# Retention moved beside its gate's block, its gated output kept in the gate's tiles, banks' release estimated, delays set anew

## Chip, core and metric

One core of a Trainium2 chip runs the whole program. The metric is the device time of one execution in microseconds (us), the median of several runs. PE is TensorE (matmuls), DVE is VectorE, ACT is ScalarE, POOL is GpSimd, SP issues most DMAs.

## The reference

Two layers over x (512 tokens x 1024). Each layer normalises h, projects it, runs four mixers of 512 columns, gates each with silu of a projection of its own, and adds the out-projection of all four to h. All is float32.

```python
for l in range(DEPTH):
    u = rmsnorm(h, norm_w[l])
    ret_p, diff_p, ssd_p, ml_p = split_cols(u @ w_in[l], (RET_COLS, DIFF_COLS, SSD_COLS, MLSTM_COLS))
    ret_out  = retention_mixer(rope(rq), rope(rk), rv) * silu(rz)     # chunks of 128 tokens, a state between
    diff_out = diff_attention_mixer(dq, dk, dv, lam) * silu(dz)
    ssd_out  = _rms(ssd_mixer(conv(xbc), dt) * silu(sz)) * ssd_norm_w
    ml_out   = mlstm_mixer(conv(mqk), mv, mo, gates) * silu(mz)       # its gates by a scan over 4 chunks
    h = h + concat([ret_out, diff_out, ssd_out, ml_out]) @ w_out[l]
return rmsnorm(h, final_norm_w)
```

## The kernel before

**Tiles.** Tokens lie in 4 tiles (t) of 128 on the partitions. Every weight block of 512 columns is loaded (`raw`) and split into a high part (`whi`, made by ACT, L327) and a low rest (`wlo`, made by DVE, L329). A product is three matmuls: `whi` with the high part of the other operand, `whi` with its low part, `wlo` with its high part. A projection block (`proj_tok`, `proj_feat`) is 96 matmuls of 128x512 in 4 PSUM tiles `pspj`; `uh`, `ul` are the parts of the normalised input, `mh`, `ml` those of a mixer's transposed output, which the out-projection (`out_proj`) multiplies. Such a block is called by its name: `rz` is the projection of retention's gate, `s` the out-projection of the SSD mixer, and so on.

**Order on PE.** PE's order is written out by the program itself, and Tile's scheduler orders the other engines. `drive` runs through the blocks in the order of the list `ORDER`. A clock `self.clk` advances by an estimate with every matmul. The mixers and their finishers are generators that are put beside the blocks: what they yield (a delay out of the table `W`) says after how much of that clock their next piece is put between the block's groups of three matmuls. `pause(key)` holds one until `key` is in the set `done`. The delays thus stand for the time that DVE, ACT and POOL take between two pieces on PE; if a delay is too short for what they take, PE waits.

**Banks.** PSUM has 8 banks. `free` puts a bank back with the clock at which its last reader was issued, and `psum` takes the one with the earliest such time. A matmul that gets a bank whose reader has not run yet waits for it.

**The pieces that the change touches.**
- Mixer mLSTM: `gates` scans over 4 chunks and transposes what DVE made (L695, L696; delays g1 to g4). `mlstm` starts m0 after the block `mk`; for each chunk a score matmul (`psS<-ft,ft`), a decay product on DVE (L760 by ACT to L767), then after mB the value matmuls (`psacc<-v,w`).
- SSD: score product on DVE (L874), value matmuls, then `fin_s`: normalised on DVE (L933), after sF the transposes.
- Differential attention (`diff`): a head's output lies in bank `o`; its last reader is L1106, and after dF its transposes follow.
- Retention (`ret`): for each chunk scores, decay product (L958), after rC the value matmuls, squares (L1002), a reciprocal root on POOL (L217), scaling (L1010). Its finisher `fin` multiplies by the gate on POOL (L842) into the w tile `mix`, and after rF `emit` transposes it on PE into a bank `psS`, and `finish_mix` makes `mh` (L547, ACT) and `ml` (L548, DVE) of that, which lie in 4 buffers each: the first tile of `r` takes those of the first tile of `s`.

Retention stands behind `rz` in `ORDER`, so its four chunks lie between the matmuls of the blocks `s` and `r`.

Of the kernel before, what the change touches and what calls it, by code (L numbers as in the profile page):

```python
# [15 lines left out]
ALU = mybir.AluOpType  # L16
# [5 lines left out]
NT = S // P  # L22
# [23 lines left out]


ORDER = ["mv", "gates", "mq", "mk", "mlstm", "mo", "mz", "dk", "dq", "diff", "dv", "dz", "m", "xs", "bc", "ssd", "d",
         "rqk", "sz", "rv", "rz", "ret", "s", "r"]


QS = 4


W = {'norm': 9.0, 'g1': 1.5, 'g2': 7.3, 'g3': 1.8, 'g4': 10.4, 'mB': 1.8, 'mC': 1.3, 'mN': 5.0, 'mF': 9.6, 'sB': 10.2,
     'sN': 0.0, 'sF': 6.1, 'rC': 2.3, 'rN': 0.0, 'rF': 9.8, 'dT': 9.14, 'dN': 1.0, 'dM': 3.0, 'dV': 6.68, 'dF': 15.46,
     'm0': 5.3, 's0': 8.8, 'dT1': 0.6, 'dN1': 1.0, 'hp': 100, 'he': 100, 'hr': 50, 'hd': 50, 'dS': 4.7, 'dQ': 6.0,
     'ha': 50}


# [31 lines left out]
class Trunk:  # L92
# [81 lines left out]
        self.bank[id(p)] = p, b  # L174
        return p

    def free(self, *ps):

        for p in ps:
            q, b = self.bank.pop(id(p))  # L180
            assert q is p
            heapq.heappush(self.banks, (self.clk, b))


    def setup(self):
# [235 lines left out]
    def proj_tok(self, name, evac, w=None, toks=range(NT), order=None):  # L421
        w = w or self.load_block(name)
        steps = [(t, k, parts) for t in toks for k, parts in order] if order else \
                [(t, k, (0, 1)) for t, k in self.steps_of(list(toks), name != "mv")]
        banks, n = {}, {}
        for t, k, parts in steps:
            if t not in banks:
                yield from self.wait(("u", self.l, t))
                banks[t] = self.psum("pj")
                n[t] = 0  # L430
            p = banks[t]
            ts_ = slice(t * P, (t + 1) * P)
            for part in parts:
                for u in (self.uh,) if part else (self.uh, self.ul):
                    n[t] += 1
                    self.mm(p, lhsT=u[:, k, ts_], rhs=w[k][part], start=(n[t] == 1), stop=(n[t] == 3 * KD))
            yield
            if n[t] == 3 * KD:
                evac(t, p)
                self.free(p)  # L440
                self.done.add((name, self.l, t))

    def proj_feat(self, name, evac):
        w = self.load_block(name)
        banks = {}
        for f, k in self.steps_of(range(4), True):
            p = banks[f] if k else banks.setdefault(f, self.psum("pj"))
            fs = slice(f * P, (f + 1) * P)
            hi, lo = w[k][0][:, fs], w[k][1][:, fs]
            self.mm(p, lhsT=hi, rhs=self.uh[:, k, :], start=(k == 0), stop=False)  # L450
            self.mm(p, lhsT=hi, rhs=self.ul[:, k, :], start=False, stop=False)
            self.mm(p, lhsT=lo, rhs=self.uh[:, k, :], start=False, stop=(k == KD - 1))
            yield
            if k == KD - 1:
                evac(f, p)
                self.free(p)


    def ev_silu(self, dst, tag, bufs, nwt=None):
# [81 lines left out]
    def finish_mix(self, mix):  # L541

        nc = self.nc
        p = self.tr4([mix[:, j * P:(j + 1) * P] for j in range(4)])
        mh = self.t("mh", [P, 512], F32R, bufs=4)
        ml = self.t("ml", [P, 512], F32R, bufs=4)
        nc.scalar.copy(out=mh, in_=p)  # L547
        nc.vector.tensor_tensor(out=ml, in0=p, in1=mh.bitcast(F32), op=ALU.subtract)  # L548
        self.free(p)
        return mh, ml  # L550

    def out_proj(self, g, mixt, tok_outer=False, after=None, cut=False, heads=False):
        nc = self.nc
        gi = GROUPS[g]
        w = [[x for q in range(2) for x in self.split_w(self.wout[self.l, gi, half, :, 2 * q:2 * q + 2, :], 2 * half + q)]
             for half in range(2)]
        l = self.l
        order = [(t, hf) for t in range(NT) for hf in range(2)] if tok_outer else \
                [(t, hf) for hf in range(2) for t in range(NT)]
        for t, hf in order:  # L560
            if hf == 0 or not tok_outer:
                yield from self.wait((g, l, t))
            m = lambda t, k: [x[:, t * P:(t + 1) * P] for x in mixt[k]] if heads else \
                [x[:, k * P:(k + 1) * P] for x in mixt[t]]
            cuts = self.cuts if cut and t == NT - 1 else (0, 512, D)
            for c0, c1 in zip(cuts, cuts[1:]):
                if c0 // 512 != hf:
                    continue
                bank = self.psum("pj")
                p = bank[:, 0:c1 - c0]  # L570
                cs = slice(c0 - hf * 512, c1 - hf * 512)
                for k in range(4):
                    hi, lo = w[hf][k]
                    mh, ml = m(t, k)
                    self.mm(p, lhsT=mh, rhs=hi[:, cs], start=(k == 0), stop=False)
                    self.mm(p, lhsT=ml, rhs=hi[:, cs], start=False, stop=False)
                    self.mm(p, lhsT=mh, rhs=lo[:, cs], start=False, stop=(k == 3))
                    yield
                hs = self.h[t][:, c0:c1]
                nc.vector.tensor_tensor(out=hs, in0=p, in1=hs, op=ALU.add)  # L580
                self.free(bank)
            if tok_outer and hf == 1:
                self.spawn(after(t))

# [157 lines left out]
    def mlstm(self, v, th, zs, q, k, res):  # L742
# [5 lines left out]
        for t in range(NT):  # L748
# [16 lines left out]
                self.mm(s[:, h * P:(h + 1) * P], lhsT=k[h][:, ts_], rhs=q[h][:, ts_])  # L765
            pt = self.pg()
            nc.vector.scalar_tensor_tensor(pt, s, sc, w, ALU.mult, ALU.mult)  # L767
            self.free(s)
            if t < NT - 1:
                kt = self.tr4([k[h][:, ts_] for h in range(4)])  # L770
                kw = self.pg()
# [1 line left out]
                                               kt.rearrange("p (h d) -> p h d", h=4), sc,  # L773
                                               self.bc(self.ws[:, t, :], P), ALU.mult, ALU.mult)
                self.free(kt)
            yield W["mB"]
            yield from self.pause(("mo", l, t))
            num = [self.psum("acc"), self.psum("acc")]
            for h in range(4):
# [25 lines left out]
            for j in range(2):  # L805
                nc.vector.scalar_tensor_tensor(g[:, j * 256:(j + 1) * 256].rearrange("p (h e) -> p h e", h=2),
                                               th[t][:, j * 256:(j + 1) * 256].rearrange("p (h e) -> p h e", h=2),
                                               1.0, nv[j][:, :, 0:128], ALU.add, ALU.mult)
            self.free(*num)
            r = self.sm([P, 4])  # L810
            nc.vector.tensor_tensor(out=r, in0=den, in1=self.em[:, t, :], op=ALU.max)
            nc.vector.reciprocal(out=r, in_=r)
# [24 lines left out]
        yield W["mF"]  # L837
        self.emit(l, t, "m", mix, res)

    def fin(self, l, t, g, mix, res, zs, key, w):  # L840
        yield from self.pause((key, l, t))
        self.nc.gpsimd.tensor_tensor(out=mix, in0=mix, in1=zs[t], op=ALU.mult)  # L842
        yield w
        self.emit(l, t, g, mix, res)


    def ssd(self, xs, bm, cm, zs, res):
# [5 lines left out]
        for t in range(NT):  # L853
# [12 lines left out]
            for g in range(2):  # L866
# [8 lines left out]
                                        in1=cb[:, g * P:(g + 1) * P].unsqueeze(1).to_broadcast([P, 4, P]),  # L875
                                        op=ALU.mult)
                es.append(e)
            self.free(cb)
            if t < NT - 1:
                pb = self.tr4([bm[g][:, ts_] for g in range(2)])  # L880
                bt = self.t("bt", [P, 256], bufs=2)
# [56 lines left out]
    def retention(self, qk, v, zs, res):  # L938
# [6 lines left out]
        for t in range(NT):  # L945
# [64 lines left out]
                nc.vector.tensor_tensor(out=v4(mix)[:, j::2, :], in0=ob[j][:, 0:256].rearrange("p (h d) -> p h d", h=2),  # L1010
                                        in1=self.bc(f[:, j::2], P), op=ALU.mult)
            self.free(*ob)
            self.spawn(self.fin(l, t, "r", mix, res, zs, "rz", W["rF"]))
            yield W["rN"]


# [11 lines left out]
    def diff(self, q, k, v, zs, res):  # L1028
        nc = self.nc
        l = self.l  # L1030
        for h in range(4):
# [6 lines left out]
            for t in range(NT):  # L1038
                n = (t + 1) * P
                ts_ = slice(t * P, n)  # L1040
                nm = self.sm([P, 2])
                pe = [self.pg(), self.pg()]
                sj = [self.psum("S"), self.psum("S")]

                for i, (a, b) in enumerate(((0, 0), (0, 1), (1, 0))):
                    for j, s in enumerate(sj):
                        own = slice(j * 64, j * 64 + 64)
                        self.mm(s[:, 0:n], lhsT=qp[a][own, ts_], rhs=k[h][b][own, 0:n], start=(i == 0), stop=(i == 2),
                                share=0.5)
                with self.tc.high_priority(W["hd"]):  # L1050
                    for j, s in enumerate(sj):
                        nc.vector.tensor_tensor(out=s[:, ts_], in0=s[:, ts_], in1=self.mlow, op=ALU.add)  # L1052
                        nc.vector.tensor_reduce(out=nm[:, j:j + 1], in_=s[:, 0:n], axis=AX.X, op=ALU.max, negate=True)  # L1053
                        nc.scalar.activation(pe[j][:, 0:n], s[:, 0:n], AF.Exp, bias=nm[:, j:j + 1],  # L1054
                                             accum_out=r[:, t, j:j + 1])
                        self.free(s)
                    rr = self.sm([P, 1])
                    nc.vector.reciprocal(out=rr, in_=r[:, t, 1:2])
                    nc.vector.scalar_tensor_tensor(ca[:, t:t + 1], rr, r[:, t, 0:1], self.nlam, ALU.mult, ALU.mult)
                    a = pe[0]  # L1060
                    nc.vector.scalar_tensor_tensor(a[:, 0:n], pe[1][:, 0:n], ca[:, t:t + 1], pe[0][:, 0:n],
                                                   ALU.mult, ALU.add)
                self.spawn(self.diff_av(l, t, h, a, o, v), W["dT"] + t * W["dT1"])
                yield W["dN"] + t * W["dN1"]
# [21 lines left out]
    def diff_fin(self, h, o, r, zs, res, l):  # L1086
# [6 lines left out]
        for t in range(NT):  # L1093
# [11 lines left out]
        mix = self.pg()  # L1105
        nc.vector.tensor_tensor(out=mix.rearrange("p (t d) -> p t d", t=NT), in0=o.rearrange("p (t d) -> p t d", t=NT),  # L1106
                                in1=self.bc(f, P), op=ALU.mult)
        self.free(o)
        for t in range(NT):
            yield from self.pause(("dz", l, t))  # L1110
            ts_ = slice(t * P, (t + 1) * P)
# [169 lines left out]
```

## Time and profile before

| what | value |
|---|---|
| median of 3 runs | 1050.69 us (1049.36 to 1051.6) |
| profiled execution | 1054.91 us, its span 1053.1 us |
| PE busy | 1024.8 us, 97% of the span |
| DVE, ACT, POOL busy | 701.9, 470.6, 192.7 us |
| mean granted clock of PE | 0.993 |

The span is what the trace shows; 1.8 us of the profiled execution lie around it. A busy PE is one with a matmul in it, at whatever clock. Layer 0 ends its last out-projection at about 535 us; the places of layer 1 lie some 516 us behind those of layer 0.

### The profile page before, as it was taken

The page shows a single profiled execution, that of the slowest core. Times are in us where ns is not written, and L with a number is a line of the kernel's source. Part 1 is how long each engine was busy: PE and PEld are TensorE (multiplying, and loading weights), DVE is VectorE, ACT ScalarE, POOL GpSimd, SP SyncE. Part 2 cuts the span into 40 slices and gives each one's busy share as a digit, 9 for nine tenths or more (in the row PEclk, how much of TensorE's full clock was granted, in tenths as well). Part 3 has the DMA queues.
Part 4 walks back from the last instruction along what each step waited for, and adds up shares of the span by engine and source line. Part 5 has one row for each costly group of instructions (what it writes and reads, how often), then busy time and mean ns, then how long its engine had stood idle before and what let it go on. Part 6 is the DMA issues. An engine that isn't in the chain of part 4 may idle for free.

```text
span 1053.1 us, 14255 instructions
## 1 busy us (share of the span) xinstructions
PE 1024.8 (97%) x5116; PEld 835.5 (79%) x5116; DVE 701.9 (67%) x1501; ACT 470.6 (45%) x1050; POOL 192.7 (18%) x221
## 2 busy tenths in 40 slices
PE   7999999999999999999999999999999999999997
PEld 6778888877778888787887788887777878888876
DVE  5587686567787868445556867666686786872554
ACT  4444336645455344432353443475444453643322
POOL 3000152102111342004000013320121112510121
PEclk8999999999999999999999999999999999999999
DMA  7323322322212332431122423223231223232202
GB/s 294 106 79 113 101 66 86 100 81 81 79 42 92 101 89 89 128 106 65 40 81 81 125 82 96 80 80 102 70 104 46 80 84 117 85 113 83 80 21 81
DMA packets 39143, 95.54 MB, mean 91 GB/s; under 512 B 3592, under 2 KB 16520, under 8 KB 38944
## 3 DMA queue, kind: packets, MB, share of 16 engines
q1 hardware_dynamic: 38064, 93.18, 28.5%
q10 hardware_dynamic: 1008, 1.44, 0.4%
q8 instruction: 40, 0.66, 0.3%
q14 instruction: 31, 0.25, 0.1%
HBM read 92.47 MB, written 2.15 MB: 90 GB/s over the span
## 4 chain that ended last, share of the span: by engine, by line
PE 85%; DVE 7%; DMA 3%; ACT 2%; issue 1%; POOL 0%; SPq 0%; POOLq 0%; DVEq 0%; ACTq 0%
PE pspj L114 70%; PE psacc L114 6%; PE psS L114 5%; PE psS L118 4%; DMA raw<-in_w_in_dram 2%; DVE wlo L329 2%; DVE e L509 1%; DVE s L1053 1%; ACT whi L327 1%; DMA cst<-in_consts_dram 1%; ACT w L1054 1%; DMA raw<-in_w_out_dram 0%; DVE h L580 0%; POOL s L217 0%; DVE psS L1052 0%
## 5 line engine op out<-in xcount | busy, mean ns | idle before, releaser
L329 DVE TENSOR_TENSOR wlo<-raw,whi 128x512 fp32r<-128x512 f32 x298 | 215.2, 740 | 69.5 <-ACT whi L327 67.1
L327 ACT CAST whi<-raw 128x512 fp32r<-128x512 f32 x300 | 178.6, 619 | 112.1 <-PE pspj L114 53.9
L114 PE MATMUL pspj<-whi,uh 128*128 128x512 f32 x512 | 208.2, 407 | 0.9 <-ACT whi L327 0.6
L114 PE MATMUL pspj<-whi,ul 128*128 128x512 f32 x512 | 200.9, 392 | 0.0
L114 PE MATMUL pspj<-wlo,uh 128*128 128x512 f32 x512 | 200.4, 393 | 0.0
L114 PE MATMUL pspj<-uh,whi 128*128 128x512 f32 x448 | 179.5, 401 | 0.0
L114 PE MATMUL pspj<-uh,wlo 128*128 128x512 f32 x448 | 174.8, 390 | 0.0
L114 PE MATMUL pspj<-ul,whi 128*128 128x512 f32 x448 | 174.7, 390 | 0.0
L114 PE MATMUL pspj<-whi,mh 128*128 128x512 f32 (+1 forms) x260 | 107.6, 414 | 8.0 <-DVE ml L548 4.2
L114 PEld LDWEIGHTS pspj<-whi,uh 128*128 128x128 f32 x512 | 97.0, 189 | 23.0 <-issue 2.0
L114 PEld LDWEIGHTS pspj<-wlo,uh 128*128 128x128 f32 x512 | 96.7, 189 | 21.0
L114 PEld LDWEIGHTS pspj<-whi,ul 128*128 128x128 f32 x512 | 97.1, 190 | 18.0
L114 PE MATMUL pspj<-whi,ml 128*128 128x512 f32 (+1 forms) x260 | 103.1, 396 | 0.2 <-DVE ml L548 0.2
L114 PE MATMUL pspj<-wlo,mh 128*128 128x512 f32 (+1 forms) x260 | 102.8, 395 | 0.0
L114 PEld LDWEIGHTS pspj<-uh,wlo 128*128 128x128 f32 x448 | 84.1, 188 | 18.3
L114 PEld LDWEIGHTS pspj<-uh,whi 128*128 128x128 f32 x448 | 84.3, 188 | 17.1 <-issue 0.7
L114 PEld LDWEIGHTS pspj<-ul,whi 128*128 128x128 f32 x448 | 84.3, 188 | 15.8
L217 POOL TENSOR_TENSOR s<-s,nhalf 128x4 f32<-128x4 f32 (+1 forms) x44 | 36.1, 820 | 328.1 <-DVE s L1101 126.5
L509 DVE SCALAR_TENSOR_TENSOR e<-pspj,cvh,e 128x511 f32<-128x511 f32 (+2 forms) x90 | 67.0, 745 | 14.3 <-ACT e L507 13.2
L114 PEld LDWEIGHTS pspj<-whi,mh 128*128 128x128 f32 x260 | 49.6, 191 | 21.3 <-issue 5.0
L580 DVE TENSOR_TENSOR h<-pspj,h 128x512 f32<-128x512 f32 (+1 forms) x65 | 43.6, 676 | 33.9 <-PE pspj L114 33.6
L527 ACT ACTIVATE e<-pspj 32x512 f32<-32x512 f32 x96 | 56.6, 589 | 19.3 <-PE pspj L114 18.0
(213 smaller groups left out, 1359.0 us busy)
## 6 DMA issues: line engine op xcount, KB each, us to landing
raw<-in_w_in_dram SPq DMA_DIRECT2D x118, 512.0 KB, 3.9
raw<-in_w_out_dram SPq DMA_DIRECT2D x32, 512.0 KB, 3.4
bcm<-adr SPq DMA_DIRECT2D x16, 256.0 KB, 3.9
bcm<-gdr SPq DMA_DIRECT2D x8, 256.0 KB, 3.4
out_dram<-z SPq DMA_DIRECT2D x7, 256.0 KB, 2.0
h<-in_x_dram SPq DMA_DIRECT2D x3, 512.0 KB, 7.9
rows<-in_rows_dram SPq DMA_DIRECT2D x2, 592.0 KB, 9.0
cst<-in_consts_dram SPq DMA_DIRECT2D x1, 1035.0 KB
```

Source lines behind the costliest of these rows:

```text
L114: self.nc.tensor.matmul(out, lhsT=lhsT, rhs=rhs, start=start, stop=stop, **kw)
L118: self.nc.tensor.transpose(out, src, self.ident if ident is None else ident)
L217: self.nc.gpsimd.tensor_tensor(out=out, in0=m, in1=self.nhalf[:, :n], op=ALU.pow)
L327: (nc.vector.tensor_copy if vector else nc.scalar.copy)(out=hi, in_=raw)
L329: eng.tensor_tensor(out=lo, in0=raw, in1=hi.bitcast(F32), op=ALU.subtract)
L509: nc.vector.scalar_tensor_tensor(acc[:, s:], p[:, 0:S - s], w[:, 3 - s:4 - s], acc[:, s:], ALU.mult, ALU.add)
L527: nc.scalar.activation(x[q * 32:q * 32 + 32, :], p[o * 32:o * 32 + 32, :], AF.Copy, scale=scale)
L580: nc.vector.tensor_tensor(out=hs, in0=p, in1=hs, op=ALU.add)
L1053: nc.vector.tensor_reduce(out=nm[:, j:j + 1], in_=s[:, 0:n], axis=AX.X, op=ALU.max, negate=True)
L1054: nc.scalar.activation(pe[j][:, 0:n], s[:, 0:n], AF.Exp, bias=nm[:, j:j + 1], accum_out=r[:, t, j:j + 1])
```

## The change

`ret` stands before `rz` in `ORDER`, so that retention's chunks lie between the matmuls of `rz`. Its gated output is written into the gate's own tile (`zs[t]`, a z tile) instead of staying in a w tile; `fin_r` waits for the gate and then for a new mark, set when the out-projection `s` has issued its last group of token tile t, before it transposes. `free` takes a `lag`, an estimate of how long after the issue of its last reader a bank is really empty: 1.0 without a word, and 1.5 to 6.0 where given. Eight delays are new, among them mB3, for the last mLSTM chunk alone.

```diff
-         "rqk", "sz", "rv", "rz", "ret", "s", "r"]
+         "rqk", "sz", "rv", "ret", "rz", "s", "r"]
...
-W = {... 'g4': 10.4, 'mB': 1.8, ... 'sF': 6.1, ... 'rN': 0.0, 'rF': 9.8, ... 'dF': 15.46, 'm0': 5.3
+W = {... 'g4': 12.4, 'mB': 1.8, 'mB3': 3.0, ... 'sF': 7.3, ... 'rN': 3.0, ... 'dF': 14.0, 'm0': 6.4
...
-    def free(self, *ps):
+    def free(self, *ps, lag=1.0):
...
-            heapq.heappush(self.banks, (self.clk, b))
+            heapq.heappush(self.banks, (self.clk + lag, b))
...
+            if hf == 1:
+                self.done.add(("used " + g, l, t))
             if tok_outer and hf == 1:
...
-            yield W["mB"]
+            yield W["mB" if t < NT - 1 else "mB3"]
...
-    def fin(self, l, t, g, mix, res, zs, key, w):
-        yield from self.pause((key, l, t))
-        self.nc.gpsimd.tensor_tensor(out=mix, in0=mix, in1=zs[t], op=ALU.mult)
-        yield w
-        self.emit(l, t, g, mix, res)
+    def fin_r(self, l, t, mix, res, zs):
+
+        yield from self.pause(("rz", l, t))
+        self.nc.gpsimd.tensor_tensor(out=zs[t], in0=mix, in1=zs[t], op=ALU.mult)
+        yield from self.pause(("used s", l, t))
+        self.emit(l, t, "r", zs[t], res)
...
-            self.free(o)
+            self.free(o, lag=6.0)
```

The other lags: proj_tok 1.5, proj_feat 3.0, finish_mix 1.5, mLSTM scores 2.0 and values 2.0, SSD scores 3.0, attention scores 2.5.

Both programs have the same matmuls, 4361 rows on PE; the following places show how the order changes. A name's number tells tiles of one kind apart, and differs between the programs.

PE, layer 0, before: in the third chunk of retention, beside `s`, stand the transposes of the first gated token tile (`psS_4650`), of which `mh_4655` is made, the fifth tile in 4 buffers:

```order
L114 MATMUL psacc_4618<-state_4569,cbs_4587 128x128
L114 MATMUL psacc_4619<-state_4569,cbs_4587 128x128
L114 MATMUL psS_4628<-v_4248,bt_4599 64x128 x4
L118 MATMUL psS_4650<-cst,w_4519 128x128 x4
L114 MATMUL psS_4663<-ft_3656,ft_3785 128x128
L114 MATMUL psS_4664<-ft_3656,ft_3785 128x128
```

Also before, 28 rows further on, `s` goes on from its first token tile (`mh_4003`, the first of the same 4 buffers) to its second (`mh_4076`) and opens the PSUM tile `pspj_4730`:

```order
L114 MATMUL pspj_4682<-wlo_4456,mh_4003 128x512
L114 MATMUL pspj_4682<-whi_4459,mh_4003 128x512
L114 MATMUL pspj_4682<-whi_4459,ml_4004 128x512
L114 MATMUL pspj_4682<-wlo_4460,mh_4003 128x512
L114 MATMUL pspj_4730<-whi_4445,mh_4076 128x512
L114 MATMUL pspj_4730<-whi_4445,ml_4077 128x512
```

In the change the same place of `s` reads as follows (`mh_4024` and `mh_4079` are its first two token tiles), and the transposes take the gated tile `z_4402`:

```order
L114 MATMUL pspj_4698<-wlo_4638,mh_4024 128x512
L114 MATMUL pspj_4712<-whi_4623,mh_4079 128x512
L114 MATMUL pspj_4712<-whi_4623,ml_4080 128x512
L114 MATMUL pspj_4712<-wlo_4624,mh_4079 128x512
L118 MATMUL psS_4716<-cst,z_4402 128x128 x4
L114 MATMUL pspj_4712<-whi_4627,mh_4079 128x512
L114 MATMUL pspj_4712<-whi_4627,ml_4080 128x512
```

The transposes have moved from ahead of the last use of `mh_4003` to behind the last use of its counterpart `mh_4024`; 35 rows of `s` lie between them and the first matmul of `r`.

PE, layer 0, the last transposes of the mLSTM gates (`cst,w_606`), before:

```order
L114 MATMUL pspj_734<-uh_66,whi_710 128x512
L114 MATMUL pspj_734<-ul_67,whi_710 128x512
L114 MATMUL pspj_734<-uh_66,wlo_711 128x512
L118 MATMUL psS_747<-cst,w_606 128x96 x4
L114 MATMUL pspj_734<-uh_66,whi_716 128x512
L114 MATMUL pspj_734<-ul_67,whi_716 128x512
L114 MATMUL pspj_734<-uh_66,wlo_717 128x512
L114 MATMUL pspj_768<-uh_66,whi_696 128x512
L114 MATMUL pspj_768<-ul_67,whi_696 128x512
L114 MATMUL pspj_768<-uh_66,wlo_697 128x512
```

And in the change:

```order
L114 MATMUL pspj_734<-uh_66,wlo_711 128x512
L114 MATMUL pspj_734<-uh_66,whi_716 128x512
L114 MATMUL pspj_734<-ul_67,whi_716 128x512
L114 MATMUL pspj_734<-uh_66,wlo_717 128x512
L114 MATMUL pspj_750<-uh_66,whi_696 128x512
L114 MATMUL pspj_750<-ul_67,whi_696 128x512
L114 MATMUL pspj_750<-uh_66,wlo_697 128x512
L114 MATMUL pspj_734<-uh_66,whi_720 128x512
L114 MATMUL pspj_734<-ul_67,whi_720 128x512
L114 MATMUL pspj_734<-uh_66,wlo_721 128x512
L118 MATMUL psS_757<-cst,w_606 128x96 x4
```

Nine matmuls of the block have moved ahead of the transposes; DVE's order up to them is the same in both.

DVE, layer 0, up to the decay product of the last mLSTM chunk (L767 of before, L769 of the change; L760 and L762 are its four parts), before:

```order
L829 TENSOR_SCALAR w_1317<-w_1317,s_372_1324,s_374_1337 128x128 x2
L467 SCALAR_TENSOR_TENSOR z_1346<-e_1344,pspj_1227 128x512
L760 SCALAR_TENSOR_TENSOR w_1387<-bcm_1376,g_147_578,cap 128x128 x4
L467 SCALAR_TENSOR_TENSOR z_1402<-e_1400,pspj_1274 128x512
L767 SCALAR_TENSOR_TENSOR w_1398<-psS_1393,w_1387 128x512
```

And in the change:

```order
L831 TENSOR_SCALAR w_1325<-w_1325,s_374_1332,s_376_1345 128x128 x4
L467 SCALAR_TENSOR_TENSOR z_1378<-e_1376,pspj_1243 128x512
L762 SCALAR_TENSOR_TENSOR w_1397<-bcm_1386,g_147_578,cap 128x128 x4
L329 TENSOR_TENSOR wlo_1530<-raw_1527,whi_1529 128x512
L769 SCALAR_TENSOR_TENSOR w_1408<-psS_1403,w_1397 128x512
```

The gate tile z of the second token tile now stands ahead of the four parts, where that of the first stood, and a split of a weight lies just ahead of the product; on PE 15 matmuls of the block lie between the chunk's scores and its value matmuls, before 9.

## Rows read from the trace of the kernel before

**Rows 1.** Page, busy time of the engines (us, share); splits of weights (busy, mean ns)
```profile
PE 1024.8 (97%) x5116; PEld 835.5 (79%) x5116; DVE 701.9 (67%) x1501; ACT 470.6 (45%) x1050; POOL 192.7 (18%) x221
...
L329 DVE TENSOR_TENSOR wlo<-raw,whi 128x512 fp32r<-128x512 f32 x298 | 215.2, 740 | 69.5 <-ACT whi L327 67.1
```

**Rows 2.** Waits of PE: what it waited for, us in total, times, longest
```profile
PE pspj L114 <- DVE ml L548: 4.5, 3, 2.1
PE pspj L114 <- DVE w L1106: 2.2, 2, 1.1
...
PE psacc L114 <- DVE w L767: 1.8, 2, 1.0
PE psS L118 <- DVE w L696: 1.7, 2, 0.9
PE psS L118 <- DVE w L933: 1.7, 2, 1.0
...
PE psS L114 <- DVE ft L514: 1.4, 2, 0.8
PE psS L118 <- DVE w L695: 1.1, 2, 0.5
...
PE pspj L114 <- ACT w L1054: 0.5, 2, 0.3
```

**Rows 3.** Windows (window: us, busy PE, PEld, DVE, ACT, POOL, granted clock, DMA)
```profile
447.00:468.00 21.00, 21.00 (x94) 17.40 (x93) 7.29 (x11) 6.82 (x13) 0.00 (x0) 1.00 0.27 90
...
498.45:501.70 3.25, 3.25 (x9) 2.57 (x8) 0.55 (x1) 0.55 (x1) 0.00 (x0) 0.51 0.00 0
...
1014.40:1017.00 2.60, 2.60 (x7) 1.98 (x6) 0.00 (x0) 0.00 (x0) 0.00 (x0) 0.50 0.00 0
...
71.00:75.00 4.00, 2.62 (x14) 1.79 (x13) 3.89 (x10) 1.78 (x4) 0.00 (x0) 1.00 0.51 157
```

**Rows 4.** Timeline, second half of `s`: start, duration, instruction, idle before and its releaser
```profile
494.08 0.40 PE L114 MATMUL pspj<-whi,ml 128*128 128x512 f32 x1
494.31 0.40 PE L114 MATMUL pspj<-wlo,mh 128*128 128x512 f32 x1
...
494.74 0.59 ACT L547 CAST mh<-psS 128x512 fp32r<-128x512 f32 x1 [1.55 <-PE pspj L114]
...
495.99 0.68 DVE L548 TENSOR_TENSOR ml<-psS,mh 128x512 fp32r<-128x512 f32 x1
496.82 0.47 PE L114 MATMUL pspj<-whi,mh 128*128 128x512 f32 x1 [2.11 <-DVE ml L548]
```

**Rows 5.** Timeline, last chunk of mLSTM
```profile
137.25 3.46 DVE L760 SCALAR_TENSOR_TENSOR w<-bcm,g,cap 128x128 f32<-128x128 f32 x4
...
141.96 0.69 DVE L467 SCALAR_TENSOR_TENSOR z<-e,pspj 128x512 f32<-128x512 f32 x1 [1.24 <-ACT e L465]
...
143.16 1.38 DVE L329 TENSOR_TENSOR wlo<-raw,whi 128x512 fp32r<-128x512 f32 x1
```

**Rows 6.** Timeline, start of the out-projection `m`
```profile
252.61 0.69 DVE L1106 TENSOR_TENSOR w<-psacc,s 128x512 f32<-128x512 f32 x1
...
253.44 0.47 PE L114 MATMUL pspj<-whi,mh 128*128 128x512 f32 x1 [1.09 <-DVE w L1106]
...
253.81 0.28 DVE L1077 COPY w<-psS 128x128 f32<-128x128 f32 x1
```

**Rows 7.** Timeline, ahead of the last SSD chunk's value matmuls
```profile
394.98 1.52 DVE L531 TENSOR_TENSOR ft<-ft,e 128x512 f32<-128x512 f32 x1 [1.18 <-POOL e L530]
395.45 1.14 ACT L327 CAST whi<-raw 128x512 fp32r<-128x512 f32 x2 [0.94 <-DMA raw<-in_w_in_dram]
...
404.43 1.27 DVE L874 TENSOR_TENSOR w<-w,psS 128x512 f32<-128x512 f32 x2
```

**Rows 8.** Timeline, last chunk of retention in layer 0
```profile
489.06 0.75 DVE L958 TENSOR_TENSOR w<-psS,cst 128x256 f32<-128x256 f32 x2
...
490.32 1.05 PE L114 MATMUL psacc<-v,w 128*128 128x128 f32 x8
```

More of the change, by code (lines that the diff above doesn't have):

```diff
@@ L48 @@
 ORDER = ["mv", "gates", "mq", "mk", "mlstm", "mo", "mz", "dk", "dq", "diff", "dv", "dz", "m", "xs", "bc", "ssd", "d",
-         "rqk", "sz", "rv", "rz", "ret", "s", "r"]
+         "rqk", "sz", "rv", "ret", "rz", "s", "r"]
 QS = 4
-W = {'norm': 9.0, 'g1': 1.5, 'g2': 7.3, 'g3': 1.8, 'g4': 10.4, 'mB': 1.8, 'mC': 1.3, 'mN': 5.0, 'mF': 9.6, 'sB': 10.2,
-     'sN': 0.0, 'sF': 6.1, 'rC': 2.3, 'rN': 0.0, 'rF': 9.8, 'dT': 9.14, 'dN': 1.0, 'dM': 3.0, 'dV': 6.68, 'dF': 15.46,
-     'm0': 5.3, 's0': 8.8, 'dT1': 0.6, 'dN1': 1.0, 'hp': 100, 'he': 100, 'hr': 50, 'hd': 50, 'dS': 4.7, 'dQ': 6.0,
+W = {'norm': 9.0, 'g1': 1.5, 'g2': 7.3, 'g3': 1.8, 'g4': 12.4, 'mB': 1.8, 'mB3': 3.0, 'mC': 1.3, 'mN': 5.0, 'mF': 9.6, 'sB': 10.2,
+     'sN': 0.0, 'sF': 7.3, 'rC': 2.3, 'rN': 3.0, 'dT': 9.14, 'dN': 1.0, 'dM': 3.0, 'dV': 6.68, 'dF': 14.0,
+     'm0': 6.4, 's0': 8.8, 'dT1': 0.6, 'dN1': 1.0, 'hp': 100, 'he': 100, 'hr': 50, 'hd': 50, 'dS': 4.7, 'dQ': 6.0,
      'ha': 50}
@@ L439, in proj_tok @@
                 evac(t, p)
-                self.free(p)
+                self.free(p, lag=1.5)
                 self.done.add((name, self.l, t))
@@ L455, in proj_feat @@
                 evac(f, p)
-                self.free(p)
+                self.free(p, lag=3.0)
     def ev_silu(self, dst, tag, bufs, nwt=None):
@@ L548, in finish_mix @@
         nc.vector.tensor_tensor(out=ml, in0=p, in1=mh.bitcast(F32), op=ALU.subtract)
-        self.free(p)
+        self.free(p, lag=1.5)
         return mh, ml
@@ L767, in mlstm @@
             nc.vector.scalar_tensor_tensor(pt, s, sc, w, ALU.mult, ALU.mult)
-            self.free(s)
+            self.free(s, lag=2.0)
             if t < NT - 1:
@@ L808, in mlstm @@
                                                1.0, nv[j][:, :, 0:128], ALU.add, ALU.mult)
-            self.free(*num)
+            self.free(*num, lag=2.0)
             r = self.sm([P, 4])
@@ L877, in ssd @@
                 es.append(e)
-            self.free(cb)
+            self.free(cb, lag=3.0)
             if t < NT - 1:
@@ L1012, in retention @@
             self.free(*ob)
-            self.spawn(self.fin(l, t, "r", mix, res, zs, "rz", W["rF"]))
+            self.spawn(self.fin_r(l, t, mix, res, zs))
             yield W["rN"]
@@ L1055, in diff @@
                                              accum_out=r[:, t, j:j + 1])
-                        self.free(s)
+                        self.free(s, lag=2.5)
                     rr = self.sm([P, 1])
```

## Prediction

> **What bounds the kernel now.** First the page: PE has a matmul in it for 1024.8 of the span's 1053.1 us [rows 1], and both programs have the same matmuls. So I cost no engine's busy time. What can change is the time in which PE stands still, and that in which it runs at half clock. Next the list of PE's waits [rows 2], in which nearly every row is a place that occurs once in each layer. A row's sum is idle time. What a wait costs is more: a matmul of 0.39 us lets the next one start 0.23 us after it, as from 494.08 to 494.31 [rows 4], so idle time is counted from 0.16 us later than the loss. The reader sees that there: behind 494.31 the next start was due at 494.54, it comes at 496.82, 2.28 late, and the row shows 2.11 idle. So a wait costs its idle time plus 0.16 us, 0.32 for a place in both layers. Last I looked at the granted clock behind each wait. Behind the longest, 2.11 us, it falls to 0.51, which is the 1.2 GHz level, for a stretch of 3.25 us, in layer 1 for 2.60 us at 0.50 [rows 3, 4].
>
> **Retention.** The longest wait is no wait for a product. The first tile of `s` ends with the matmul at 494.31; only then does ACT write `mh` at 494.74, and DVE `ml` from 495.99 to 496.67 [rows 4]. These two are retention's first finished tile, the fifth in four buffers, so they wait until `s` has read its first tile for the last time. Their source is the bank of transposes that stand before that. The next group of `s` got this bank, because it had been put back as the earliest, and stands at 496.82. In the change the transposes follow the mark "used s", so the buffer is free when they are issued, and the lag of 1.5 keeps the bank back. I take the wait and the half clock as gone: 2 x (2.11 + 0.16) = 4.5 us, and half of the slow stretches, 0.5 x (3.25 + 2.60) = 2.9 us, together **-7.4 us**. Below, it cannot give less than 4.5 if the order is as built; the stretches come back only behind another wait as long.
>
> What a shorter wait does to the clock matters below: around the gates' waits, of up to 0.9 and 0.5 us close behind each other [rows 2], the clock stayed at 1.00 from 71 to 75 us [rows 3]. The Trainium skill, in "TensorE: Matmul & The Clock Gate", section "A second HAM failure mode: psum-queue depth-cycling", tells of a kernel in which PE's short stops at banks between groups of matmuls were enough to make the clock swing between its levels. By that page every new wait at a bank would cost some 1.5 us more, which the row does not bear out at this size; it stands among the rivals with a small chance (rival 2).
>
> What retention now stands beside: `rz`, whose matmuls cover as many matmuls between a chunk's scores and value matmuls as those of `s` did. In the last chunk of before the decay product ran from 489.06 to 489.81 and the value matmuls began at 490.32 [rows 8], so 0.51 us were to spare. Beside `rz` DVE also has the weights' splits and the z evacuations. A split takes 0.74 us in the mean [rows 1], and up to 1.38 [rows 5], so a slow one ahead of the product costs 1.38 - 0.51 = 0.87 us. By DVE's order this threatens the last chunk alone, which has splits and an evacuation ahead of it. Bounds: nothing to 0.87 a layer; the splits are there but mean ones nearly fit, so half, **+0.9 us** for both layers. The two pauses of `fin_r` hold no engine: they say behind which matmuls the transposes stand, and POOL's product, which these read, is then made beside `rz`, a whole block earlier. On POOL the next chunk's root L217 stands behind that product; it has the time from one chunk to the next, some 5 us at 35 to 40 rows of PE.
>
> **Delays.** *g4* puts the gates' last transposes nine matmuls later, 9 x 0.23 = 2.1 us. The longest waits there are 0.9 and 0.5, 1.4 and 0.32 with the restarts, so 2.1 covers them; the sums of both layers are 1.7 and 1.1 [rows 2]. DVE's order up to there is unchanged. Gone: 2.8 + 4 x 0.16, rounded down since two of the restarts lie among short matmuls: **-3.3 us**. *m0* puts the first mLSTM scores three matmuls, 0.69 us, later; they wait 1.4 us in both layers [rows 2], so 1.7 with the restarts, of which 2 x 0.69 go: **-1.4 us**. *sF* puts the SSD transposes six matmuls, 1.4 us, later, against waits of at most 1.0 [rows 2]: 1.7 + 0.32, **-2.0 us**. The lag on the attention scores takes another bank for the group of the out-projection that waits for L1054: 0.5 + 0.32 [rows 2], **-0.8 us**.
>
> *mB3* gives the last mLSTM chunk six matmuls more, 1.4 us, against waits of 1.8 in both layers, 2.1 with the restarts [rows 2]. By that alone all of it goes. But DVE's order now has the second gate tile ahead of the four parts (L760) instead of behind them, and a split of a weight ahead of the product. That tile was made from 141.96 to 142.65, and the parts took 3.46 us [rows 5]. Bounds: nothing is left of the wait, -2.1; or the parts begin only at 142.65 and the product after 146.1, while the value matmuls' turn is at 143.39 - 0.9 + 1.4 = 143.9: 2.2 plus the product's own 0.7, 2.9 a layer, 5.8 in both, so +3.7. I take the middle, **+0.8 us**, since nothing tells how much of the parts' time was waiting between them.
>
> **Lags.** They only choose among banks. One choice looks bad: the lag of 6.0 on `o`. The out-projection `m` starts at 253.44, waiting for L1106, which ends at 253.30 [rows 6]. With `o` held back, its first group gets a bank whose reader is the copy L1077, two DVE instructions later, 253.81 to 254.09 [rows 6]. So it starts 0.79 us later in each layer, **+1.6 us**. Its idle time is then 1.09 + 0.79 = 1.88 us, nearer to the 2.11 that brought the clock down than to the 0.84 that did not [rows 3]: I put it at one layer of two, 1.5 us, **+1.5 us**. Bounds: nothing (another bank) to 1.6 + 2 x 1.5. dF, 1.46 shorter, puts a head's transposes earlier; the list has no wait for their source now, so I cost it at nothing; without that slack each of eight heads would lose up to 1.46.
>
> *SSD, last chunk.* DVE's order there now takes two splits ahead of L531. That add waited for POOL at 394.98 and ran 1.52 us; the two whi that the splits need come from ACT from 395.45 to 396.59 [rows 7]. The second split can so begin at about 396.6 and end at 397.3, the add at about 398.0, 1.5 us later than now at 396.50; the splits it took ahead are later missing (2 x 0.68 us), so the score product L874, which now starts at 404.43, just in time, comes 0.2 to 1.2 us late. Middle, 0.7 in each layer: **+1.4 us**.
>
> All else: POOL's product into z is the same instruction with another target; the w tile that it no longer holds frees a buffer earlier, which I cost at nothing, since PE hides it; without that cover it would be a wait for a w tile on DVE, of which PE's waits show none.
>
> **Sum.** -7.4 - 3.3 - 1.4 - 2.0 - 0.8 + 0.9 + 0.8 + 1.6 + 1.5 + 1.4 = -8.7 us, from 1054.91 to 1046.2 in the profiled execution. That one lies 4.2 us above the median 1050.69; the profile's rows are differences, so I carry the -8.7 over: **1042.0 us**.
>
> **Rivals.**
> 1. *The new waits stay small* (mLSTM's last chunk gone, -2.1 instead of +0.8; SSD and retention's last chunk nothing; no half clock behind `m`): -7.4 - 3.3 - 1.4 - 2.0 - 0.8 - 2.1 + 1.6 = -15.4, 1035.3 at the best, mostly 1036 to 1040. For it: each cover has grown by the delays; against it: DVE's orders.
> 2. *The new waits bring the clock down.* Half clock behind `m` in the second layer too and once behind the last mLSTM chunk (+3.0), three more chunks of retention waiting 0.87 (+2.6): -3.1, 1047.6, with fewer or more of them 1046 to 1049. For it: the stretches of rows 3 followed idle times that one more DVE instruction would give.
> 3. *Slower: retention is late beside* `rz`. If in each of the eight chunks a slow and a fast split (1.38 + 0.69) stand ahead of the decay product, with 0.51 to spare, each waits 1.56 us, 12.5 in all, against the 8.7 + 0.9 that the rest gives: +2.9, 1053.6. It decides from 9.6 / 8 = 1.2 us a chunk. Against it: in a stretch of `rz` before, DVE is busy for 7.29 of 21.00 us [rows 3], and its order has the splits ahead of the product only in the last chunk.
> 4. *The wait in* `s` *does not go* (another bank, read late, is taken again): -8.7 + 7.4 = -1.3, 1049.4, no change to speak of.
>
> **Numbers.** Forecast 0.57 (1040 to 1046), rival 1 0.18, rival 2 0.13, rival 3 0.05, rival 4 0.07. Leaving out rivals 3 and 4 and the best of rival 1: 1036.5 to 1049. A run of this kernel tells about 0.2%, 2.1 us, from no change: faster below 1048.6, so all of the forecast, of rival 1 and most of rival 2, 0.84; slower above 1052.8, 0.05; between 0.11.
>
> **What would show it.** Right: PE's waits have no row for `ml` L548 of some 2 us, none for L695 and L696, and no window at 0.5 in `s`; `m` starts behind L1077 (L1079 there) with about 1.9 idle; the last mLSTM chunk still waits for its product; the rows for the SSD score product appear with 0.5 to 1.2. Wrong: waits of PE for the decay product in every chunk beside `rz`, or a half clock stretch in `rz`.

## The result and the profile after

The changed kernel takes 1041.62 us (median of 6 runs, 1039.28 to 1043.39), the kernel before 1051.21 in the same comparison: a ratio of 0.9904, 95% interval 0.9891 to 0.9916. The forecast was 1042.0. The profiled execution took 1043.25 us, with a span of 1041.2, against 1054.91.

First the page of the changed kernel, its line on busy time:

```profile
PE 1021.6 (98%) x5116; PEld 834.7 (80%) x5116; DVE 703.6 (68%) x1501; ACT 471.8 (45%) x1050; POOL 193.2 (19%) x221
```

PE has the same matmuls and is busy for 3.2 us less than in [rows 1]; the rest of the 11.9 us of span went from its idle time. The 3.2 us are not taken apart here. One part lies where the change touches nothing: in the trace of before PE also ran at half clock at the start of the program, between 20 and 24 us, and in the changed kernel's it did not. The same window of both, before and after (columns as in [rows 3]):

```profile
22.00:24.00 2.00, 2.00 (x6) 1.57 (x6) 0.81 (x3) 1.08 (x4) 0.60 (x2) 0.56 0.59 225
```

```profile
22.00:24.00 2.00, 2.00 (x10) 1.47 (x9) 1.20 (x4) 2.00 (x7) 0.20 (x1) 1.00 0.65 252
```

Which idle time went, the list of PE's waits shows (all of it; us in total, times, longest):

```profile
PE pspj L114 <- DVE w L1080: 3.6, 2, 1.8
PE psS L118 <- DMA cst<-in_consts_dram: 3.1, 1, 3.1
PE psacc L114 <- DVE w L769: 2.6, 2, 1.3
PE psS L118 <- DVE e L305: 1.6, 1, 1.6
PE psS L114 <- DVE ones L198: 1.0, 1, 1.0
PE pspj L114 <- DVE whi L327: 0.6, 1, 0.6
PE pspj L114 <- ACT whi L327: 0.3, 1, 0.3
```

Of the rows in [rows 2] two are left, and both have grown: the start of `m`, now behind L1080 (L1077 of before), 3.6 against 2.2, and the last mLSTM chunk, 2.6 against 1.8. Gone are `ml` L548, the gates' two, the SSD transposes, the first mLSTM chunk and the attention scores. The other rows lie in the first 21 us of the program, which the change doesn't touch; the wait for the constants, 3.1 us here, was 1.9 to 3.9 in the profiles of this study.

Where the wait in `s` was [rows 4], the timeline of the changed kernel now shows this:

```profile
492.94 0.60 PE L118 MATMUL psS<-cst,z 128*128 128x128 f32 x4
...
493.58 0.58 ACT L547 CAST mh<-psS 128x512 fp32r<-128x512 f32 x1 [3.53 <-PE psS L118]
...
494.20 0.69 DVE L548 TENSOR_TENSOR ml<-psS,mh 128x512 fp32r<-128x512 f32 x1 [1.05 <-ACT mh L547]
```

ACT's copy begins as soon as the transposes end, where it had waited for a buffer, and DVE's follows at once: the bank is empty 1.4 us after the transposes' end.

The start of `m` (timeline) and the granted clock around it in both layers (windows):

```profile
251.29 0.28 DVE L1080 COPY w<-psS 128x128 f32<-128x128 f32 x1
...
251.63 0.50 PE L114 MATMUL pspj<-whi,mh 128*128 128x512 f32 x1 [1.78 <-DVE w L1080]
```

```profile
252.90:256.00 3.10, 3.10 (x10) 2.45 (x9) 3.10 (x4) 0.35 (x1) 1.68 (x2) 0.50 0.29 112
...
760.50:763.80 3.30, 2.67 (x7) 2.11 (x8) 2.90 (x6) 2.28 (x7) 3.22 (x6) 0.64 0.59 187
```

The idle time of 1.78 us is 0.1 from the 1.88 forecast, and the clock falls behind it in both layers, not in one.

The last mLSTM chunk of the changed kernel, against [rows 5]:

```profile
137.32 0.69 DVE L467 SCALAR_TENSOR_TENSOR z<-e,pspj 128x512 f32<-128x512 f32 x1 [1.84 <-ACT e L465]
137.93 3.49 DVE L762 SCALAR_TENSOR_TENSOR w<-bcm,g,cap 128x128 f32<-128x128 f32 x4
...
138.09 1.34 POOL L1154 TENSOR_TENSOR z<-z,rows 128x512 f32<-128x512 f32 x1 [3.46 <-DVE z L467]
...
139.51 1.29 POOL L838 TENSOR_TENSOR w<-w,z 128x512 f32<-128x512 f32 x1
...
140.76 2.25 POOL L758 TENSOR_TENSOR w<-w,ft 128x128 f32<-128x128 f32 x4
...
141.34 0.95 DVE L329 TENSOR_TENSOR wlo<-raw,whi 128x512 fp32r<-128x512 f32 x1
141.45 0.63 ACT L764 ACTIVATE w<-w 128x512 f32<-128x512 f32 x1 [1.41 <-DVE w L762]
...
142.21 0.68 DVE L769 SCALAR_TENSOR_TENSOR w<-psS,w 128x512 f32<-128x512 f32 x1
...
142.94 0.49 PE L114 MATMUL psacc<-v,w 128*128 128x129 f32 x2 [1.28 <-DVE w L769]
```

The four parts begin only behind the second gate tile at 137.32 and take 3.49 us, while POOL works beside them almost throughout. ACT's exponential waits for them and ends at 142.08. The split of a weight then still runs on DVE, to 142.29, and the product comes right behind it. One part alone took 0.34 us earlier in the kernel (79.84 in the trace of before), here 0.87 in the mean; no run takes POOL's work away, so its share in that is not shown.

### The profile page after: what moved, and what is told of

Its sections match the earlier page's. It is cut to its first block, busy times and chain, and to the rows that moved or that the text cites. A ratio compares the mean times of both kernels' runs of the same rounds, so it can differ in the third digit from the quotient of the medians.

```text
span 1041.2 us, 14256 instructions
## 1 busy us (share of the span) xinstructions
PE 1021.6 (98%) x5116; PEld 834.7 (80%) x5116; DVE 703.6 (68%) x1501; ACT 471.8 (45%) x1050; POOL 193.2 (19%) x221
## 4 chain that ended last, share of the span: by engine, by line
PE 95%; DVE 3%; DMA 1%; ACT 1%; issue 0%; POOL 0%; SPq 0%; POOLq 0%; DVEq 0%; ACTq 0%
PE pspj L114 79%; PE psacc L114 6%; PE psS L114 6%; PE psS L118 4%; DVE wlo L329 1%; DMA cst<-in_consts_dram 1%; DVE w L762 1%; DVE z L467 0%; DVE s L1056 0%; ACT e L230 0%; ACT whi L327 0%; DVE e L305 0%; DVE z L1221 0%; DVE w L769 0%; DVE h L580 0%
## 5 line engine op out<-in xcount | busy, mean ns | idle before, releaser
L329 DVE TENSOR_TENSOR wlo<-raw,whi 128x512 fp32r<-128x512 f32 x298 | 212.0, 730 | 61.9 <-ACT whi L327 55.8
L114 PEld LDWEIGHTS pspj<-whi,mh 128*128 128x128 f32 x260 | 49.6, 191 | 15.3 <-DVE w L1080 4.4
```

The source lines that it names most:

```text
L114: self.nc.tensor.matmul(out, lhsT=lhsT, rhs=rhs, start=start, stop=stop, **kw)
L329: eng.tensor_tensor(out=lo, in0=raw, in1=hi.bitcast(F32), op=ALU.subtract)
```

## The experiments

All ratios are to the kernel before, run beside it on the same chip (its medians: 1051.2 to 1052.6 us). The experiments ran on three chips, so where a time is set against the changed kernel's 1041.62 us, differences of about 1 us say little. Waits and clock come from each run's profile. Of the seven entries of the table of delays that the diff changes (not eight), rN is tested with the place, and dF has no run of its own; rF only falls away with `fin`.

**The mark alone.** The kernel before, retention still behind `rz` in the order and so beside `s`; no lag, no new delay.

```diff
+            if hf == 1:
+                self.done.add(("used " + g, l, t))
...
-        self.nc.gpsimd.tensor_tensor(out=mix, in0=mix, in1=zs[t], op=ALU.mult)
-        yield w
-        self.emit(l, t, g, mix, res)
+        self.nc.gpsimd.tensor_tensor(out=zs[t], in0=mix, in1=zs[t], op=ALU.mult)
+        yield from self.pause(("used s", l, t))
+        self.emit(l, t, g, zs[t], res)
```

> The kernel before, with retention still beside s, but its finisher waits for the mark 'used s' and writes into the z tile; no lags, no new delays. Theory A (PE stood in s because the first gated tile's transposes lay in a bank whose copies waited for buffers that s still read): the wait of 2.1 us for ml and the half clock behind it go in both layers, -7.4 us against before, about 1043.5. Theory B (retention needs the cover of rz): the waits stay or come back as waits for the decay product or the gated tile, less than 2 us gained.

Measured 1044.84 us, 0.9931 (0.9915 to 0.9947), which is 7.3 us. No wait for `ml`, no half clock in `s`; all other waits as before.

**The whole of the retention part.** As above, with `ret` ahead of `rz` and rN at 3.0.

```diff
-         "rqk", "sz", "rv", "rz", "ret", "s", "r"]
+         "rqk", "sz", "rv", "ret", "rz", "s", "r"]
-     'rN': 0.0
+     'rN': 3.0
```

> The kernel before with the whole of the retention part (order, fin_r, mark, rN) and nothing else. Theories A and B both: -7.4 us against before. Only if moving the chunks beside rz costs or gives something of its own does this differ from the run with the mark alone: A says by less than 1 us; B says this one is the faster by over 5 us.

Measured 1046.38 us, 0.9942 (0.9927 to 0.9957): 1.5 us more than the mark alone, on the same chip. The intervals of the two overlap, but the traces show a cost. The same 442 matmuls of layer 0, none of them with a wait in the list, take 82.94 us with the mark alone (438.24 to 521.18) and 83.81 here (437.76 to 521.58); a like stretch of layer 1 takes 82.12 and 83.00. With rN at 0.0 the end of a chunk and the scores of the next stand together (first fence, the mark alone); with rN at 3.0 matmuls of the block lie between them (second fence, this run):

```profile
473.66 0.66 PE L114 MATMUL psS<-v,bt 128*64 128x128 f32 x8
474.24 0.71 PE L114 MATMUL psS<-ft,ft 64*128 64x128 f32 x8
```

```profile
460.93 0.66 PE L114 MATMUL psS<-v,bt 128*64 128x128 f32 x8
461.52 0.50 PE L114 MATMUL pspj<-whi,uh 128*128 128x512 f32 x1
...
465.14 0.72 PE L114 MATMUL psS<-ft,ft 64*128 64x128 f32 x8
```

The block is broken into three times more in each layer (13 times in that stretch of layer 0, not 10), which makes 0.29 us for a break and 1.7 us for both layers. So the place with rN at 3.0 adds nothing to the mark and costs these 1.7 us.

**The bank alone.** The kernel before, the same order on PE, and only one bank held back.

```diff
-        self.free(p)
-        return mh, ml
+        self.free(p, lag=8.0)
+        return mh, ml
```

> The kernel before, with a lag of 8.0 on the bank of finish_mix alone; the order on PE is the same, retention's early transposes stay. If the bank by itself is what stops PE (the copies for ml may wait as long as they like, as nobody needs them yet): -7.4 us, no wait for ml. If the held copies also hold up what stands behind them on ACT and DVE, or the next banks are late too: a wait of over 1 us elsewhere in s, less than half of the gain.

Measured 1044.82 us, 0.9927 (0.991 to 0.9943), and no wait for `ml`. The longest rows of its list:

```profile
PE psS L118 <- DMA cst<-in_consts_dram: 3.2, 1, 3.2
PE pspj L114 <- DVE w L1106: 2.2, 2, 1.1
```

So the late copies harmed nobody by being late; what stopped PE was only that the next group of `s` took their bank.

**The lags alone.** The kernel before with all lags of the change, the order on PE unchanged.

```diff
-    def free(self, *ps):
+    def free(self, *ps, lag=1.0):
...
-            heapq.heappush(self.banks, (self.clk, b))
+            heapq.heappush(self.banks, (self.clk + lag, b))
```

> The kernel before with the lags of the change alone; the order on PE is the same. Theory 1: a lag of 1.5 on finish_mix keeps retention's bank back far enough, -7.4 us, the attention scores' lag gives -0.8, the start of m loses 1.4 and up to 2.9 by half clock: -6.8 to -3.9 us. Theory 2: 1.5 is too short for a bank that is held for 8 us, the wait in s stays: +0.6 to +3.5 us.

Measured 1050.44 us (12 runs), 0.9995 (0.9984 to 1.0006). Its waits of PE:

```profile
PE pspj L114 <- DVE ml L548: 4.2, 2, 2.1
...
PE pspj L114 <- DVE w L1077: 3.6, 2, 1.8
```

The wait in `s` stays, as theory 2 has it: 1.5 is too short for a bank that is full, in the trace of before, from the transposes at 486.20 to the end of `ml` at 496.67. The start of `m` grows to 1.8, so this loss is the lags' own. The time is below the 0.6 to 3.5 us of loss that theory 2 gave: in this profile the clock stayed at full level behind all four waits, which the forecast had not allowed for. One profile may not stand for all: eight of the 12 runs, the profiled one (1049.61) among them, took 1048.9 to 1050.7 us, the other four 1052.1 to 1053.9.

**The delays alone.** The kernel before with g4, m0, sF and mB3.

```diff
-  'g4': 10.4, 'mB': 1.8,               'sF': 6.1, 'm0': 5.3
+  'g4': 12.4, 'mB': 1.8, 'mB3': 3.0,   'sF': 7.3, 'm0': 6.4
```

> The kernel before with g4, m0, sF and mB3 of the change alone. By the terms: gates -3.3, first mLSTM chunk -1.4, SSD transposes -2.0, last mLSTM chunk +0.8, together -5.9 us, some 1046. Rival (the waits were only cover for something that is late next): less than half of that.

Measured 1044.33 us, 0.9928 (0.9916 to 0.9941), 7.5 us, where 5.9 was expected. Its waits:

```profile
PE pspj L114 <- DVE ml L548: 4.2, 2, 2.1
...
PE psacc L114 <- DVE w L767: 2.6, 2, 1.3
PE pspj L114 <- DVE w L1106: 2.2, 2, 1.1
```

The gates, the first mLSTM chunk and the SSD transposes are gone; the last mLSTM chunk has grown to the 2.6 of the changed kernel. So the delays make that loss without help from retention or lags; that it is mB3, and not g4 or m0 ahead of it, is not shown by itself.

**The place, in the changed kernel.** Retention behind `rz` again, everything else as changed; then the same with rN at 0.0.

```diff
-         "rqk", "sz", "rv", "ret", "rz", "s", "r"]
+         "rqk", "sz", "rv", "rz", "ret", "s", "r"]
```

> The changed kernel with retention back behind rz in the order, so that its chunks lie beside s again; the mark, the z tile, lags and delays stay. If the place is worth nothing (the mark alone gave -7.3 us, the mark with the place -6.1 on the kernel before): within 1 us of the changed kernel. If the place is worth something beside the other delays: some us slower, with waits in s or r.

Measured 1048.01 us, 0.9964 (0.9949 to 0.9978). The timeline shows the last token tile, finished too late for the transposes that begin `r`, and the half clock behind it (matmuls of 0.63):

```profile
501.91 1.26 POOL L845 TENSOR_TENSOR z<-w,z 128x512 f32<-128x512 f32 x1 [1.07 <-DVE w L1013]
...
503.23 1.12 PE L118 MATMUL psS<-cst,z 128*128 128x128 f32 x4 [2.62 <-POOL z L845]
504.00 0.78 PE L114 MATMUL pspj<-whi,mh 128*128 128x512 f32 x1
504.57 0.63 PE L114 MATMUL pspj<-whi,ml 128*128 128x512 f32 x1
```

> The changed kernel with retention beside s again and rN at 0.0, as the kernel before has both. With rN at 3.0 it lost 5 to 6 us to waits for the gated z tile and a half clock. If it is rN that made the last token tile late there: within 1 us of the changed kernel, no wait for z. If it is the place: as slow as with rN 3.0.

Measured 1040.86 us, 0.9891 (0.9879 to 0.9904), no wait for z. So it was rN: with the chunks 3.0 further apart they don't fit beside `s`. Moving retention makes room for the longer rN, and the two together give nothing: without them the kernel is as fast or faster, and the trace has the 0.9 us a layer of the breaks less (82.96 against 83.81 us for the same stretch, 82.10 against 83.00 in layer 1). Retention beside `rz` with the old rN was not run.

**The lag of `o`, at 1.0.** The changed kernel with one number changed.

```diff
-        self.free(o, lag=6.0)
+        self.free(o)
```

> The changed kernel with the lag of o back at 1.0. Theory: the start of the out-projection m takes the bank of o again and waits for the scaling product as before, idle 1.1 instead of 1.8 us, and without the half clock behind it: -1.4 and -2.9, together -4.3 us against the changed kernel, some 1037.3. Rival (the clock falls there for another reason, or another late bank is taken): within 1 us of the changed kernel.

Measured 1065.01 us, 1.0121 (1.0101 to 1.014): 23 us slower than the changed kernel, where 4.3 faster was expected. Its waits:

```profile
PE pspj L114 <- ACT w L1057: 6.7, 2, 3.3
PE psS L118 <- ACT w L1057: 6.6, 2, 3.3
PE psS L114 <- DVE w L1109: 6.1, 2, 3.1
```

All three are waits for the bank of an `o`, also where the row names ACT's L1057. In layer 0:

```profile
247.06 0.69 DVE L1109 TENSOR_TENSOR w<-psacc,s 128x512 f32<-128x512 f32 x1
...
247.90 0.30 PE L118 MATMUL psS<-cst,w 128*128 128x128 f32 x1 [3.31 <-ACT w L1057]
```

L1109, the last reader of `o`, ends 0.15 us before the waiting matmul starts, here and at the two other places (277.99 for 278.14, 308.85 for 308.99). Followed through the program's own `free` and `psum`, the bank of `o` is taken again 2.6 to 3.8 of its clock after it was put back, for three heads of four, the first of them ahead of `m`. With a lag of 4.0 it is 6.7 to 8.4. The lag of 6.0 loses 0.7 us of waiting at `m` and protects these three places.

**The lag of `o`, at 4.0.** Between the two: the bank comes back behind the last group ahead of `m` and ahead of the others.

> The changed kernel with the lag of o at 4.0: short enough that the out-projection m opens with the bank of o, long enough that no group before it takes it (with 1.0 one did, and three waits of over 3 us came). Theory: idle 1.1 instead of 1.8 us at the start of m and no half clock behind it, -1.4 and -2.9, some 1037.3. Rival: the later groups, which get other banks too, wait elsewhere: gain under 1 us or a loss.

Measured 1037.85 us, 0.9869 (0.9853 to 0.9886). `m` waits for L1109, 2.2 in both layers, and no half clock behind it: 3.8 us less than the changed kernel's median, where 4.3 was expected.

**mB3 at 4.6.**

```diff
-  'mB3': 3.0
+  'mB3': 4.6
```

> The changed kernel with mB3 at 4.6: six more matmuls, 1.4 us, ahead of the last mLSTM chunk's value matmuls. If DVE's order stays, the waits of 1.3 us go: -2.8 us, some 1038.8. If more DVE work moves ahead of the product, as it did from 1.8 to 3.0, they stay at over 1 us: within 0.5 us of the changed kernel.

Measured 1039.16 us, 0.9884 (0.9868 to 0.9899); the wait for L769 is gone.

**Both together.**

> The changed kernel with the lag of o at 4.0 and mB3 at 4.6. The two gains add if they are apart: -4.3 - 2.8 = -7.1 us, some 1034.5; otherwise as the better one of the two.

Measured 1036.42 us, 0.9856 (0.9839 to 0.9873): 5.2 us less than the changed kernel, where 7.1 was expected and the two runs apart gave 3.8 and 2.5. Of the program's waits behind the start only L1109 is left, 2.2 us. In the trace POOL's root ends at 245.72, but the small product that takes it, L1107, runs only at 247.78, behind a reduction and splits, and L1109 at 249.05, behind a gate tile and one more split.

**And the scaling product at a higher priority.**

```diff
-        nc.vector.tensor_tensor(out=f, in0=f, in1=ri, op=ALU.mult)
         mix = self.pg()
-        nc.vector.tensor_tensor(out=mix..., in0=o..., in1=self.bc(f, P), op=ALU.mult)
+        with self.tc.high_priority(26):
+            nc.vector.tensor_tensor(out=f, in0=f, in1=ri, op=ALU.mult)
+            nc.vector.tensor_tensor(out=mix..., in0=o..., in1=self.bc(f, P), op=ALU.mult)
```

> The fastest version so far (lag of o 4.0, mB3 4.6) with the last two DVE instructions on an attention head's output at a higher priority, so that the scaling product stands ahead of a gate tile and a split. Theory: the out-projection m no longer waits (1.1 us idle in each layer), -2.5 us, some 1034. Rival: the gate tiles or score reductions that now stand behind it are late, and PE waits for them: no gain or a loss.

Measured 1033.98 us, 0.983 (0.9818 to 0.9843), the fastest version: 7.6 us below the changed kernel and 2.4 below the one without the priority, where 2.5 was expected. Its waits of PE, all of them, and the start of `m` in its timeline:

```profile
PE psS L118 <- DMA cst<-in_consts_dram: 3.9, 1, 3.9
PE psS L114 <- DVE ones L198: 1.1, 1, 1.1
PE psS L118 <- DVE e L305: 0.7, 1, 0.7
PE pspj L114 <- ACT whi L327: 0.3, 1, 0.3
```

```profile
247.42 0.68 DVE L1110 TENSOR_TENSOR w<-psacc,s 128x512 f32<-128x512 f32 x1
...
248.25 0.47 PE L114 MATMUL pspj<-whi,mh 128*128 128x512 f32 x1
```

Every wait that is left lies in the first 21 us.

## Why the prediction was right, and where its terms were not

| term | forecast, us | measured |
|---|---|---|
| wait and half clock in `s` | -7.4 | -7.3 (mark alone) and -7.7 (bank alone); both gone in the profile after |
| gates, g4 | -3.3 | rows gone |
| first mLSTM chunk, m0 | -1.4 | row gone, so -1.7 |
| SSD transposes, sF | -2.0 | row gone |
| attention scores' lag | -0.8 | row gone |
| last mLSTM chunk, mB3 | +0.8 | idle 2.6 against 1.8: +0.8 |
| `m`, wait | +1.6 | idle 3.6 against 2.2: +1.4 |
| `m`, half clock | +1.5 | in both layers, some 0.5 x 3.1 and 0.36 x 3.3: +2.7 |
| retention's last chunk | +0.9 | no row: 0 |
| retention's breaks with rN 3.0 | none | +1.7 (the whole part against the mark alone) |
| SSD, last chunk | +1.4 | no row: 0 |

The measured column sums to -8.6 with -7.4 for the first term; the medians give -9.6, the two profiled executions -11.7. Between -8.6 and -11.7 lie a wait of before in layer 1 that no other profile of this study has (1.06 and 0.22 us idle at 856.68 and 857.40, -1.6 with the restarts) and the start of the program (-0.5: the constants came 1.0 later, but before lost more to its half clock there; the same matmul starts at 29.93 in before and at 29.47 after). 1.0 us is left over.

The mechanism of the large terms was right. That the time came within 0.4 us of the forecast is partly luck: +2.3 us for two last chunks did not come, while 1.2 more than forecast came at `m` by the clock, and 1.7 by the breaks, which the forecast did not have at all.

**The wait in `s`.** The mechanism was as told, and the experiments show its parts apart: bank alone and mark alone each take it away. One sentence of the forecast fell: "the lag of 1.5 keeps the bank back". The run with the lags alone shows that it does not; the mark does the work, because the copies then run at once. And the part of the change that gives it its name, the place beside `rz`, gains nothing: with its rN it costs 1.7 us in the traces (1040.86 us without it, 1041.62 with it, a difference that the medians alone don't show).

**The place beside `rz`.** The term for the last chunk was mis-sized: a split and a gate tile do stand there, but the product L961 ran from 474.72 to 475.46 and the value matmuls began at 476.58 in the trace after, 1.1 us later; the splits ahead of it took 0.68 each, not 1.38. Rival 3 needed a wait of 1.2 us a chunk and got none. What the place does cost, the breaks, is in no term of the forecast: it looked for waits, and a break shows as none.

**SSD.** The forecast had DVE about right. The add L531 ended at 397.74, near the forecast 398.0, and the score product started at 404.66 against 404.43:

```profile
397.06 0.68 DVE L531 TENSOR_TENSOR ft<-ft,e 128x512 f32<-128x512 f32 x1
...
404.66 1.27 DVE L877 TENSOR_TENSOR w<-w,psS 128x512 f32<-128x512 f32 x2
...
405.63 1.89 PE L114 MATMUL psacc<-w,w 128*128 128x64 f32 x16
```

That is 0.23 later by the clock of the trace, and 1.0 later by PE's own work, which runs 0.8 us earlier here: the matmul that stands last ahead of the value matmuls in before, at 404.85, ran at 404.03. What failed is the step that leaves PE's turn where it was. Six more matmuls of the block, 1.4 us, stand ahead of the value matmuls in the changed kernel (the last at 405.39), so the later product is still in time.

**`m`.** Place, releaser and length were right. The clock was put at one layer of two, by the length of the idle time, and fell in both. The length does not settle it: with the same wait of 1.8 us the lags alone and retention beside `s` with rN 3.0 kept the full clock in both layers.

**Sums of parts.** Mark alone -7.3, delays alone -7.5 and lags alone -0.5 make -15.3, the change -9.6. The clock can account for 5.6 of the 5.7 us between them, if one profile stands for the runs of its kernel: the lags alone show no half clock in `s`, 2.9 us that the mark's gain holds as well, and none at `m`, 2.7 us that the change has. But the parts also leave out rN with the place, 1.7 us, and dF, so this sum is an account that fits and not one that is shown.

## What to carry to other kernels

A PSUM bank is not free when its last reader is issued. Where a program deals out banks by its own clock, a bank whose reader is held up by something else, here by a buffer four tiles back, stops the matmuls that happen to get it; look in the list of waits for a releaser that the waiting matmul doesn't use. The estimate has two sides: `o` at 1.0, 4.0 and 6.0 gave 1065.0, 1037.9 and 1041.6 us. Before moving a mixer to another block, try the delay or the mark that comes with the move by itself. And compare how long the same matmuls take, not only the waits.

## What the runs showed of the hardware

The clock does not always fall behind a wait of some 2 us. In the profiles of before, the changed kernel, the lags alone, the delays alone, mB3 at 4.6 and the two with retention beside `s` there are 18 waits of PE of 1.8 to 2.6 us behind the start; behind 12 the granted clock went to 0.50 for about 3 us, behind 6 it stayed at 1.00 (the four of the lags alone, and the start of `m` in both layers with retention beside `s` and rN 3.0). In these 18 the same place always did the same in both layers. The lag of `o` at 1.0 shows that this is no rule: behind its 3.31 us at the first place the clock fell in layer 0 (247.90) and stayed at 1.00 in layer 1 (769.33), and behind its four other waits, 3.05 to 3.34 us, it fell. Behind waits of up to 1.3 us it never fell. So the length of the wait alone does not decide, from 1.8 up to 3.3 us; what else does is left open here.

A break in a run of 512-column matmuls costs PE time that no list of waits shows: 0.29 us for each of the three that rN 3.0 adds in a layer, in two pairs of traces (82.94 to 83.81 and 82.96 to 83.81 us).
